# A tile of the token sums on the scan mask's place, priority for score copies, and a half-sum of the down weights moved to the branches

## The chip, the cores and the metric

The kernel runs on one core of a Trainium2 chip. TensorE (PE in the profile) multiplies matrices and writes to the PSUM banks; VectorE (DVE) and ScalarE (ACT) empty those banks and do the elementwise work; GpSimd (POOL) does elementwise work and issues part of the transfers; SyncE (SP) issues the rest. The engines run side by side and wait for each other through semaphores; each one works through its own queue strictly in order. The metric is the time of one execution on the device in microseconds; lower is better. A time "before" or "after" is a median over several runs.

## The reference

One decoder layer over 16 meta tokens and 1024 tokens of width 1024: a mixer with two branches (gated linear attention, GLA, and an mLSTM, 4 heads each) and a gated MLP with a width-3 causal convolution.

```python
def mixer_block(h, ...):
    proj = h @ w_in + b_in
    (g_q, g_k, g_v, g_r, g_lr, m_q, m_k, m_v, m_o, m_i, m_f, gate_a, gate_b) = split(proj)
    log_a = log_sigmoid(g_lr @ gla_w_gate + gla_b_gate) / GLA_TAU
    o_gla = head_rms(gla_chunked(g_q * dk**-0.5, g_k, g_v, log_a), gla_norm) * silu(g_r)
    mq, mk = split(silu(causal_dwconv(concat(m_q, m_k), ml_conv_w, ml_conv_b)))
    o_ml = head_rms(mlstm_chunked(mq * dk**-0.5, mk, m_v, m_i, log_sigmoid(m_f)), ml_norm) * sigmoid(m_o)
    y = sigmoid(gate_a) * (o_gla @ w_branch_gla) + sigmoid(gate_b) * (o_ml @ w_branch_ml)
    return y @ w_out
def conv_ffn(h, ...):
    gate, up = split(causal_dwconv(h @ w_up, conv_w, conv_b))
    return (silu(gate) * up) @ w_down
h = concat(meta, x)
h = h + mixer_block(rms_norm(h, norm_mix), ...)
h = h + conv_ffn(rms_norm(h, norm_ffn), ...)
return rms_norm(h, norm_final)[:, N_META:]
```

In the GLA scores, `scores[t, s] = sum_k q[t,k] k[s,k] exp(bc[t,k] - bc[s,k])` for `s <= t`, with `bc` the running sum of `log_a` within a chunk.

## The kernel before

**Stages.** Projections and heads first: head s = 0 to 3 is GLA, 4 to 7 mLSTM. While PE projects keys, queries and values of one head (matmuls `pj` and `pv`, lines 234, 263 and 276), the steps of the head before are mixed in as generators (`gla`, `mlstm`, then `post`). Then come the gates (`Vg`, `Xg`, `Yg`, `Zg`), the two branches (`bg`, `bm`), the output product (`po`), the second norm, the FFN's up products (`Vu` to `Zu`) and its down products (`pd`). Every matrix operand is split into a high and a low part (`wH`, `wL`; `xH`, `xL`), and three products are added.

**What sets the order.** A scheduler orders each engine's queue by priorities. `with hp(PRI_E)` raises the priority of what stands in it, mostly of the copies that empty a PSUM bank ("evictions"). `tc.issue_after(x)` puts a piece of work behind an instruction in the order. Tiles with the same tag share their buffers (`bufs` of them) in turn; a new tile waits until all users of the tile that held its buffer are done.

**Token sums.** The gates and the up product multiply block matrices with fewer products (sums of blocks are multiplied in place of single blocks). For the gates, sums of token blocks are made ahead on POOL: `token_sums(k)` writes four sums and differences into the halves of two tiles, `xa` and `xb`, and stores them to `tsc` in 8 transfers. It is called once early on (k = 0) and then in `post(4)`, `post(5)` and `post(6)`, that is while heads 5, 6 and 7 run. `xa` and `xb` have the tag `of` with two buffers, and so has `KT`, the transposed keys of a head: PE transposes keys into the banks `kt`, DVE scales them into `KT` (line 1101), and then PE's score products `msc` (line 1108) and the state updates `up` (line 1120) follow.

**The scan mask.** `rmask` (line 109) is ones with zeros at the starts of chunks. The scans that make running sums per chunk read it, last in `small_rows` (line 683), which runs beside the end of the GLA heads. After that it is not used.

**Half-sums.** `half_load` and `half_sums` (lines 644 to 658) load half a pair of rows of the down weights into a tile `ts`, make four differences on POOL and store them to `tdn`, for the down product much later. There are 22, taken in turn from the list `half`: three in `post(3)` to `post(5)`, five beside the last gates, seven in the `bg` steps, and the rest in the `bm` steps, one in each for as long as the list holds, on the place of the tiles `Y0` and `Y1` in turn. After the branches, the tokens' rows are loaded: `h1` onto `Y0` and `h2` onto `Y1` by POOL, the others by SP.

**GLA scores.** Within a chunk the score matrix is put together from halves of sizes 1, 2, 4 to 64 (`scores_small` for 1 to 16, `scores_large` for 32 and 64), and from the diagonal (`scores_diagonal`). `turn` flips the odd half by a product with `flip`. Each takes one of the three `s` banks of PSUM, whose next user waits for the copy out of it. In `small_rows`, lines 688, 692, 697 and 704 are DVE's sums on rows of 4 partitions (`sr` in the profile), and line 280 adds the bias to a projected value block (`v`), which frees a bank of `pj` and `pv`.

Of the kernel before, what the change touches and what calls it, by code (L numbers as in the profile page):

```python
# [9 lines left out]
F32 = mybir.dt.float32  # L10
F32R = mybir.dt.float32r
U8 = mybir.dt.uint8
AF = mybir.ActivationFunctionType
# [4 lines left out]
P = 128  # L18
# [3 lines left out]
T = NM + SEQ  # L22
# [23 lines left out]
def hybrid_kernel(ctx, tc, x, meta, norm_mix, w_in, b_in, gla_w_gate, gla_b_gate, gla_norm,  # L46
                  ml_conv_w, ml_conv_b, ml_norm, w_branch_gla, w_branch_ml, w_out, norm_ffn,
                  ffn_w_up, ffn_conv_w, ffn_conv_b, ffn_w_down, norm_final, out):
    nc = tc.nc
    x, out = x[0], out[0]  # L50
# [8 lines left out]
    def hp(n):  # L59

        return tc.high_priority(offset=max(1, min(n, tc.cur_priority - floor[0])))
# [9 lines left out]
    hd = heads_ctx.enter_context(tc.tile_pool(name="hd", bufs=1, side="right"))  # L71
# [32 lines left out]
    with tc.issue_after(loads[0]):  # L104
# [1 line left out]
    load_x(2)  # L106
    sent = nc.scalar.dma_start(m0[:, 1], bass.AP(tensor=norm_mix.tensor, offset=norm_mix.offset,
                                                 ap=[[P, NK], [0, NM], [1, P]]))
    rmask = hd.tile([P, T], F32, name="rmask")
    nc.vector.memset(rmask, 1.0)  # L110
    nc.vector.memset(rmask[:, 0:1], 0.0)
    nc.vector.memset(rmask[:, NM:].rearrange("p (n w) -> p n w", w=P)[:, :, 0:1], 0.0)
# [108 lines left out]
    PRI_W, PRI_E, PRI_Q, PRI_D, PRI_N = 2500, 2500, 600, 600, 400  # L221
# [92 lines left out]
    A = hd.tile([P, NC, P], F32, name="A", tag="A", bufs=1)  # L314
# [194 lines left out]
    with tc.issue_after(last.ins):  # L509

        lmask = {}
# [104 lines left out]
    def token_sums(k, queue):  # L616

        a, b = ([t[:, :514], t[:, 520:1034]] for t in (
            hd.tile([P, T], F32, name=f"x{i}{k}", tag="of", bufs=2) for i in "ab"))

        def whole(dst, i, c0):
            nc.gpsimd.tensor_tensor(dst, xH[:, i, c0:c0 + 514].bitcast(F32), xL[:, i, c0:c0 + 514].bitcast(F32), OP.add)

        def less(dst, x, y):
            nc.gpsimd.tensor_tensor(dst, x, y, OP.subtract)
        first, second = T0, T0 + 512
        whole(a[1], k, second)
        whole(a[0], k, first)
        less(b[0], a[1], a[0])
        whole(b[1], k + 4, second)  # L630
        less(a[1], b[1], a[1])
        less(b[1], b[1], b[0])
        whole(a[0], k + 4, first)
        less(a[0], a[0], b[1])
        for i, src in enumerate((b[0], b[1], a[1], a[0])):
            for p in range(2):
                stored = queue.dma_start(tsc[p][i, :, k], src[:, 258 * p:258 * p + 258 - 2 * p])
        return stored
# [15 lines left out]
    def half_sums(t, m, c):  # L654
        for o, a, b in ((0, 1, 0), (1, 3, 1), (3, 3, 0), (2, 2, 3)):
            nc.gpsimd.tensor_tensor(t[:, o], t[:, a], t[:, b], OP.subtract)  # L656
        for i in range(2):
            nc.gpsimd.dma_start(tdn[i][m][:, :, 256 * c:256 * c + 256], t[:, 2 * i:2 * i + 2])
# [71 lines left out]
    def post(s, oraw, om, sc):  # L730

        h = s % 4
        g = "g" if s < 4 else "m"
        after = rooted[0]
        if 4 <= s < 7:
            with tc.issue_after(after.ins):
                after = token_sums(s - 3, nc.gpsimd)
        for c in range(NC):
            o = oraw[c // 4][:, DV * (c % 4):DV * (c % 4 + 1)]
            nc.scalar.activation(o, o, AF.Copy, scale=sc[:, c + 1:c + 2])  # L740
        nc.scalar.activation(om, om, AF.Copy, scale=sc[:2, 0:1])
        nc.sync.dma_start(omd[g][h], om)
        for _ in range({3: 2, 6: 3}.get(s, 3)):
            yield
        dst = osc[g][2 * h:2 * h + 2].rearrange("t (q i) n -> i (t q) n", i=32)
        for j in range(2):
            t32 = hd.tile([P, T], F32, name=f"of{s}_{j}", tag="r", bufs=2)[:, :SEQ]
            with tc.issue_after(held[0]) if s > 2 else nullcontext():
                nc.vector.transpose(t32.rearrange("p (b c j) -> p c b j", b=8, c=4),
                                    oraw[j][:, :SEQ].rearrange("p (c b j) -> p c b j", c=4, b=8))  # L750
            yield
            if 3 <= s < 6:
                if j == 0:
                    with tc.issue_after(after.ins):
                        t = half_load(wp, "gst")
                else:
                    half_sums(*t)
            for a in range(4):
                nc.sync.dma_start(dst[:, :, 256 * a + P * j:256 * a + P * j + P],
                                  t32[32 * a:32 * a + 32].rearrange("p (b n) -> p b n", b=8))  # L760
            yield
# [54 lines left out]
    def gla(s):  # L816
# [7 lines left out]
        An = hd.tile([P, T], F32, name=f"An{s}", tag="of", bufs=2)  # L824
        raw = An[:, 512:SEQ]
        An = An[:, :512].rearrange("p (i t) -> p i t", t=P)
# [21 lines left out]
        def scores_diagonal(kq):  # L848

            for g in range(2):  # L850
                pt = ps.tile([P, 4, P], F32, name=f"sc{s}_0_{g}", tag="s", bufs=3)
                column_sums(pt, kq[g])
                nc.vector.copy_predicated(An if g else A.rearrange("p (i c) t -> p i c t", c=2)[:, :, 0, :],
                                          lmask[0][:, None, :].to_broadcast([P, 4, P]), pt)

        def turn():

            pt = ps.tile([P, 4, P], F32, name=f"sct{s}", tag="s", bufs=3)
            nc.tensor.matmul(pt, flip, A.rearrange("p (i c) t -> p i c t", c=2)[:, :, 1, :], start=True, stop=True)
            nc.scalar.activation(An, pt, AF.Copy)  # L860

        def products(pk, b):

# [8 lines left out]
        def scores_large(pk, b):  # L872
            m = 64 // b
            pt = products(pk, b)
            for c in range(2):
                A2 = An if c else A.rearrange("p (i c) t -> p i c t", c=2)[:, :, 0, :]
                for n in range(m):
                    p0 = b * (m * c + n)
                    nc.scalar.activation(A2[2 * b * n:2 * b * n + b, :, 2 * b * n + b:2 * b * (n + 1)],
                                         pt[p0:p0 + b, :, p0:p0 + b], AF.Copy)  # L880

        def scores_small(pk, b):
            pt = products(pk, b)
# [44 lines left out]
        for b in (1, 2, 4, 8, 16, 32, 64):  # L928
            made.append((b, level(b)))
            if len(made) > (3 if s == 0 else 2):  # L930
                c, pk = made.pop(0)
# [4 lines left out]
        if len(made) > 2:  # L936
            c, pk = made.pop(0)
# [4 lines left out]
        c, pk = made.pop(0)  # L942
# [35 lines left out]
        for g in range(2):  # L978
            tp = ps.tile([P, 4, P], F32, name=f"kt{s}_{g}", tag="s", bufs=3)
            for i in range(4):  # L980
                c = 4 * g + i
# [36 lines left out]
        for c2 in range(NC // 2):  # L1018
# [3 lines left out]
            for i in range(2):  # L1022
                c = 2 * c2 + i
# [8 lines left out]
            for i in range(2):  # L1032
                c = 2 * c2 + i
# [5 lines left out]
            for i in range(2):  # L1039
                c = 2 * c2 + i  # L1040
# [355 lines left out]
    for q in range(NG):  # L1396
        gu[q] = [row(f"gu0{q}", "u0", 2),
                 first_row if q == 1 else row(f"gu1{q}", "o1" if q % 2 else "u1")]
        for p in range(2):
            g = piece(psG, f"g{q}", p, gu[q], u2, WP[q], gate_block)  # L1400
# [85 lines left out]
    for j in END:  # L1486
        pt = prod3(ugb[j], [[t[:, k] for k in range(NK)] for t in (xH, xL)], False, f"pe{j}", 0, T0)
# [12 lines left out]
    for j in range(NK):  # L1500
# [4 lines left out]
        pt = prod3(ubg[j], og, j < 2, f"bg{j}")  # L1505
# [17 lines left out]
    for j in range(NK):  # L1523
# [7 lines left out]
        pt = prod3(ubm[j], om_, j < 1, f"bm{j}")  # L1531
# [24 lines left out]
    for t in range(NC + 1):  # L1556
        a = r2.tile([P, T], F32, name=f"h{t}", tag=f"Y{t - 1}") if t else rb.tile([P, T], F32, name="h0", tag="T12")
# [14 lines left out]
    for p in "HL":  # L1572
        t = rb.tile([P, 28, W0], F32R, name=f"B{p}0", tag=f"B{p}0")
# [213 lines left out]
    for i, tiles in enumerate(([1, 5, 2, 6, 0], [3, 7, 4, 8])):  # L1787
        for n in range(4):
# [13 lines left out]
            for it, t in enumerate(rest):  # L1802
                pt = po_bank(n, t, ("V1", "X1")[it % 2])
# [19 lines left out]
    for q in range(NJ):  # L1823
        for p in range(2):
            g = up_piece(q, p)
# [153 lines left out]
    t = r2.tile([P, 4, D], F32, name="accs", tag="OL1")  # L1979
# [121 lines left out]
    i = FIRST  # L2101
    while i < len(seq):
        r, ph, m = seq[i]
        k = i % NP2
# [3 lines left out]
        n = 4 if (r, ph, k) == (1, 1, NP2 - 4) else 2 if k in (0, NP2 - 2) else 1  # L2108
# [4 lines left out]
        if (r, ph) == (1, 0) and 2 <= k < 6:  # L2113
            scaled, x, rs = ready[k - 2]
# [46 lines left out]
```

## Time and profile before

| what | value |
|---|---|
| median of 3 runs | 1843.21 us (1843.0 to 1844.52) |
| the profiled execution | 1844.82 us |
| its span, first to last instruction | 1843.1 us |
| TensorE clock granted, mean | 0.999 |
| POOL busy in 0 to 600 us (heads) | 160.47 us |
| POOL busy in 870 to 1070 us (branches) | 100.59 us |
| PE idle in the first 40 us | 4.53 us |
| PE idle in the last 23 us | 8.2 us |

The page lists busy times per engine, the chain of work that ended last and the costliest groups of instructions. The chain goes through PE for 85% of the span, DVE for 6%, POOL, ACT and transfers for 2% each. A row of the timeline gives start, length, engine, line, operation, output and input, their shapes and how many instructions the row stands for; in brackets stands how long the engine was idle before it, and who ended that. "The old clock" is the time from the start of this profiled span.

### The profile page before, as it was taken

The numbers are of one execution on the slowest core, as the hardware profiler recorded it, in microseconds if no ns is written. First come the engines' busy times: TensorE is split into PE (matmuls) and PEld (weight loads), VectorE is DVE, ScalarE is ACT, GpSimd is POOL, SyncE is SP. The second block draws the span as 40 slices with busy tenths as digits, with TensorE's granted clock in tenths as the row PEclk, the third lists the DMA queues.
The fourth block names the chain that finished last, engine by engine and source line by source line (L and its number), as shares of the span: only waits on it lengthen the run. The fifth ranks groups of instructions, "written<-read, shape, count | busy, mean of one in ns | idle before, by whom it ended". The sixth has DMA issues, their size and how long they took to land.

```text
span 1843.1 us, 32483 instructions
## 1 busy us (share of the span) xinstructions
PE 1822.7 (99%) x13142; PEld 1756.9 (95%) x13142; DVE 1247.3 (68%) x1858; ACT 850.9 (46%) x1366; POOL 444.2 (24%) x511
## 2 busy tenths in 40 slices
PE   9999999999999999999999999999999999999998
PEld 8999999999999999999999999999999999988886
DVE  7966856656553566765613637798887887787876
ACT  6564564645434433332513235444434433465664
POOL 5400211205530011134462700013222222100100
PEclk9999999999999999999999999999999999999999
DMA  5212212224425354566963733333333334298894
GB/s 164 59 43 56 52 34 61 69 84 141 126 66 166 102 171 150 161 184 189 342 212 115 266 124 115 115 121 121 104 111 101 115 116 124 90 336 316 284 383 163
DMA packets 237469, 269.63 MB, mean 146 GB/s; under 512 B 15282, under 2 KB 194797, under 8 KB 237319
## 3 DMA queue, kind: packets, MB, share of 16 engines
q1 hardware_dynamic: 215583, 196.20, 34.4%
q0 software_dynamic: 19136, 62.62, 9.8%
q10 hardware_dynamic: 2600, 8.74, 1.3%
q8 instruction: 103, 1.69, 0.4%
q14 instruction: 47, 0.39, 0.1%
HBM read 197.91 MB, written 69.60 MB: 145 GB/s over the span
## 4 chain that ended last, share of the span: by engine, by line
PE 85%; DVE 6%; issue 3%; POOL 2%; ACT 2%; DMA 2%; SPq 0%; POOLq 0%; DVEq 0%; ACTq 0%
PE pj L234 8%; PE Yu L1218 7%; PE Zu L1218 7%; PE Xu L1218 7%; PE pv L276 5%; PE bg L1471 5%; PE bm L1471 5%; PE Zg L1218 4%; PE Yg L1218 4%; PE Xg L1218 4%; PE po L1765 4%; PE Vu L1218 3%; PE pdZ L1921 3%; PE pdX L1921 3%; PE pdY L1921 3%
## 5 line engine op out<-in xcount | busy, mean ns | idle before, releaser
L656 POOL TENSOR_TENSOR ts<-ts 128x256 f32<-128x256 f32 x88 | 81.9, 939 | 45.0 <-DMA ts<-in_ffn_w_down_dram 43.2
L1678 POOL TENSOR_TENSOR SB<-SA,rg 128x512 f32<-128x512 f32 x20 | 32.7, 1634 | 239.8 <-issue 101.4
L276 PE MATMUL pv<-wH_mv,xH 128*128 128x256 f32 x256 | 74.5, 291 | 0.1
L276 PE MATMUL pv<-wH_gv,xH 128*128 128x256 f32 x256 | 74.3, 290 | 0.0
L1765 PE MATMUL po<-wH_wo,yH 128*128 128x256 f32 x256 | 72.5, 283 | 0.1
L276 PE MATMUL pv<-wH_gv,xL 128*128 128x256 f32 x256 | 72.0, 281 | 0.0
L276 PE MATMUL pv<-wL_mv,xH 128*128 128x256 f32 x256 | 72.0, 281 | 0.0
L1765 PE MATMUL po<-wL_wo,yH 128*128 128x256 f32 x256 | 71.7, 281 | 0.3 <-DVE wL_wo L147 0.3
L276 PE MATMUL pv<-wL_gv,xH 128*128 128x256 f32 x256 | 71.9, 281 | 0.0
L276 PE MATMUL pv<-wH_mv,xL 128*128 128x256 f32 x256 | 71.9, 281 | 0.0
L1765 PE MATMUL po<-wH_wo,yL 128*128 128x256 f32 x256 | 71.8, 281 | 0.0
L1713 DVE SCALAR_TENSOR_TENSOR cv<-u,fc,cv 128x1024 f32<-128x1024 f32 x44 | 65.2, 1482 | 0.4
L920 POOL TENSOR_TENSOR pk<-pk,kT 128x256 f32<-128x256 f32 (+1 forms) x24 | 31.8, 1330 | 130.3 <-ACT pk L918 130.1
L1660 POOL TENSOR_TENSOR A<-u2raw,A 128x512 fp32r<-128x512 f32 x20 | 42.4, 2122 | 86.3 <-ACT A L1659 86.3
L1471 PE MATMUL bg<-ogL,wH_bg 128*128 128x342 f32 x192 | 61.5, 320 | 0.0
L1471 PE MATMUL bg<-ogH,wH_bg 128*128 128x342 f32 x192 | 61.5, 320 | 0.0
L1471 PE MATMUL bm<-omH,wH_bm 128*128 128x342 f32 x192 | 61.4, 320 | 0.0
L1471 PE MATMUL bm<-omH,wL_bm 128*128 128x342 f32 x192 | 61.3, 319 | 0.0
L1471 PE MATMUL bg<-ogH,wL_bg 128*128 128x342 f32 x192 | 61.3, 319 | 0.0
L1471 PE MATMUL bm<-omL,wH_bm 128*128 128x342 f32 x192 | 61.2, 319 | 0.0
L280 DVE TENSOR_TENSOR v<-pv,bB 128x256 f32<-128x256 f32 x64 | 26.6, 415 | 38.2 <-PE pv L276 38.0
L1659 ACT ACTIVATE HA<-rg 128x1024 fp32r<-128x1024 f32 x16 | 17.0, 1060 | 73.0 <-PE Yu L1218 72.6
(829 smaller groups left out, 7491.1 us busy)
## 6 DMA issues: line engine op xcount, KB each, us to landing
gw<-in_w_in_dram SPq DMA_DIRECT2D x26, 512.0 KB
ts<-in_ffn_w_down_dram POOLq DMA_DIRECT2D x44, 256.0 KB, 4.2
tdn<-ts POOLq DMA_DIRECT2D x44, 256.0 KB, 3.4
rg<-in_ffn_w_up_dram SPq DMA_DIRECT2D x22, 512.0 KB
ru<-in_ffn_w_up_dram SPq DMA_DIRECT2D x22, 512.0 KB
adr<-s SPq DMA_DIRECT2D x40, 256.0 KB
rd<-in_ffn_w_down_dram SPq DMA_DIRECT2D x20, 512.0 KB
do<-tdn SPq DMA_DIRECT2D x18, 512.0 KB
```

The source lines that it names most:

```text
L234: nc.tensor.matmul(pt[:, :n], a[:, k, :], b[:, k, base + t0:base + t0 + n], start=(i == 0), stop=(i == 3 * NK - 1))
L276: nc.tensor.matmul(pt[:, :DV], a[:, k, t0:t0 + P], b[:, k % 4, :], start=(i == 0), stop=(i == 3 * NK - 1))
L280: hold(nc.vector.tensor_tensor(vt[:n, c, :DV], pt[:n, :DV], bB[:n, :], OP.add).ins)
L656: nc.gpsimd.tensor_tensor(t[:, o], t[:, a], t[:, b], OP.subtract)
L920: eng.tensor_tensor(e, e, k, OP.mult)
L1218: nc.tensor.matmul(out[:, :n], x[:, k, :], y[:, k, :], start=start and k == 0 and j == 0, stop=stop and k == 3 and j == 2, skip_group_chec ...
L1471: nc.tensor.matmul(pt[:, i, :n], a[:, k, :], b[k][:, base + t0:base + t0 + n], start=(k == 0 and j == 0), stop=(k == NK - 1 and j == 2))
L1660: eng.tensor_tensor(l, src, h.bitcast(F32), OP.subtract)
L1678: late.tensor_tensor(sb[:, 0:4], sa[:, 0:4], rg[:, 0:4], OP.subtract)
L1713: nc.vector.scalar_tensor_tensor(y, u[:, j:SEQ + j], fc[:, j, jj:jj + 1], y, OP.mult, OP.add)
L1765: nc.tensor.matmul(pt[:, :DV], a, b[:, k % 4, :], start=(k == 0 and i == 0), stop=(k == NK - 1 and i == len(terms) - 1))
L1921: nc.tensor.matmul(banks[r, j, b][:, c], p, q[:, c], start=first and k == 0, stop=last and k == 2, skip_group_check=True)
```

## The change

Three edits; what is computed stays the same:

1. `rmask` gets a tag, `rm`, of its own with one buffer. In `token_sums(k)` with k > 0, `xb` takes that place in place of a buffer of the tag `of`; `xa` stays where it was. For k = 0 nothing changes.
2. The half-sum in `post(3)` is dropped (`3 <= s < 6` becomes `4 <= s < 6`). The list `half` keeps its 22 entries, so every later place takes the entry before, and the last step of the branches (`bm`, j = 7) now has one too, on the tile `Y1`.
3. The copies out of the banks in `turn`, `scores_diagonal` and `scores_large` get eviction priority, `hp(PRI_E)`.

```diff
-    rmask = hd.tile([P, T], F32, name="rmask")
+    rmask = hd.tile([P, T], F32, name="rmask", tag="rm", bufs=1)
...
         a, b = ([t[:, :514], t[:, 520:1034]] for t in (
-            hd.tile([P, T], F32, name=f"x{i}{k}", tag="of", bufs=2) for i in "ab"))
+            hd.tile([P, T], F32, name=f"x{i}{k}", tag=tag, bufs=2 if tag == "of" else 1)
+            for i, tag in (("a", "of"), ("b", "rm" if k else "of"))))
...
-            if 3 <= s < 6:
+            if 4 <= s < 6:
...
                 column_sums(pt, kq[g])
-                nc.vector.copy_predicated(An if g else A.rearrange("p (i c) t -> p i c t", c=2)[:, :, 0, :],
-                                          lmask[0][:, None, :].to_broadcast([P, 4, P]), pt)
+                with hp(PRI_E):
+                    nc.vector.copy_predicated(An if g else A.rearrange("p (i c) t -> p i c t", c=2)[:, :, 0, :],
+                                              lmask[0][:, None, :].to_broadcast([P, 4, P]), pt)
...
-            nc.scalar.activation(An, pt, AF.Copy)
+            with hp(PRI_E):
+                nc.scalar.activation(An, pt, AF.Copy)
...
-                    nc.scalar.activation(A2[2 * b * n:2 * b * n + b, :, 2 * b * n + b:2 * b * (n + 1)],
-                                         pt[p0:p0 + b, :, p0:p0 + b], AF.Copy)
+                    with hp(PRI_E):
+                        nc.scalar.activation(A2[2 * b * n:2 * b * n + b, :, 2 * b * n + b:2 * b * (n + 1)],
+                                             pt[p0:p0 + b, :, p0:p0 + b], AF.Copy)
```

On DVE, around the scaling of the keys of head 6 (`K0`, `A0` and `KT6` are written from the banks `k0t6` and `kt6`; in brackets stand the semaphores that a row waits for: DMASW are transfers that POOL issued), before:

```order
L749 STREAM_TRANSPOSE of5_1_5130<-or5_1_4736 128x4x8x32 [waits DMAHW6_49,DMAHW7_49,DMAHW5_49,DMAHW3_49]
L1093 TENSOR_SCALAR K0_436<-k0t6_5133,tcol_435 16x128 [waits PE_49]
L1094 TENSOR_SCALAR A0_437<-k0t6_5133,tcol_435 16x1
L1101 TENSOR_TENSOR KT6_5132<-kt6_0_5139,tcol_435 128x512 [waits DMASW1_49,DMASW6_49,DMASW0_49,DMASW7_49,PE_49,Pool_49]
L1101 TENSOR_TENSOR KT6_5132<-kt6_1_5145,tcol_435 128x512 [waits PE_49]
L147 TENSOR_TENSOR wL_mv3_1_5216<-wr_mv3_1_5213,wH_mv3_1_5215 128x1024 [waits DMAHW4_49,PE_49,Activation_49]
```

and with the change:

```order
L750 STREAM_TRANSPOSE of5_1_5121<-or5_1_4727 128x4x8x32 [waits DMAHW6_49,DMAHW7_49,DMAHW5_49,DMAHW3_49]
L1097 TENSOR_SCALAR K0_436<-k0t6_5124,tcol_435 16x128 [waits PE_49]
L1098 TENSOR_SCALAR A0_437<-k0t6_5124,tcol_435 16x1
L1105 TENSOR_TENSOR KT6_5123<-kt6_0_5130,tcol_435 128x512 [waits PE_49]
L1105 TENSOR_TENSOR KT6_5123<-kt6_1_5136,tcol_435 128x512 [waits PE_49]
L147 TENSOR_TENSOR wL_mv3_1_5207<-wr_mv3_1_5204,wH_mv3_1_5206 128x1024 [waits DMAHW4_49,PE_49,Activation_49]
```

The order of the rows stays; the first `KT6` no longer waits for transfers or for POOL. Heads 5 and 7 read the same way.

On POOL, at the end of GLA head 3 (`rs3r` is the root for its norm; `kT` and `qT` are the zeroed edges of later keys and queries), before:

```order
L700 MEMSET sr_3569 4x16
L124 TENSOR_TENSOR rs3r<-rs3v,mhalf 128x9
L650 DMA ts_3700<-in_ffn_w_down_dram 128x2x256 x2
L656 TENSOR_TENSOR ts_3700<-ts_3700 128x256 x3
L658 DMA tdn_432<-ts_3700 256x1x256
L656 TENSOR_TENSOR ts_3700<-ts_3700 128x256
L658 DMA tdn_433<-ts_3700 256x1x256
L592 MEMSET kT_4388 128x3
```

and with the change:

```order
L701 MEMSET sr_3569 4x16
L124 TENSOR_TENSOR rs3r<-rs3v,mhalf 128x9
L592 MEMSET kT_4379 128x3
L592 MEMSET kT_5047 128x3
L592 MEMSET qT_5048 128x3
```

The half-sum's two loads, four subtractions and two stores are gone from here.

On POOL, at the end of the branches (`h1` and `h2` are rows of tokens, `hr` roots of the second norm), before:

```order
L656 TENSOR_TENSOR ts100_10853<-ts100_10853 128x256
L658 DMA tdn1_433<-ts100_10853 256x1x256
L1561 DMA h1_11065<-in_x_dram 128x1024
L1561 DMA h2_11067<-in_x_dram 128x1024
L1596 TENSOR_TENSOR hr0_11574<-hv0_11572,mhalf_81 128x1
```

and with the change:

```order
L1565 DMA h1_11065<-in_x_dram 128x1024
L651 DMA ts101_11046<-in_ffn_w_down_dram 128x2x256 x2
L657 TENSOR_TENSOR ts101_11046<-ts101_11046 128x256 x3
L659 DMA tdn0_432<-ts101_11046 256x1x256
L657 TENSOR_TENSOR ts101_11046<-ts101_11046 128x256
L659 DMA tdn1_433<-ts101_11046 256x1x256
L1565 DMA h2_11067<-in_x_dram 128x1024
L1600 TENSOR_TENSOR hr0_11574<-hv0_11572,mhalf_81 128x1
```

A half-sum now stands between the two loads, and `h2` waits for its stores, since it takes the same place.

## The prediction

> **What bounds the kernel now.** I read the page first, for the engine that has no slack.
>
> ```profile
> span 1843.1 us, 32483 instructions
> PE 1822.7 (99%) x13142; PEld 1756.9 (95%) x13142; DVE 1247.3 (68%) x1858; ACT 850.9 (46%) x1366; POOL 444.2 (24%) x511
> ```
>
> PE works 1822.7 of 1843.1 us, and the change leaves every matmul in place. So only PE's idle 20.4 us can be won, and a loss can only be a new idle stretch of PE. The table of waits, for PE alone, says who makes it idle (us in total, times, longest):
>
> ```profile
> PE msc L1108 <- DVE KT L1101: 2.9, 2, 2.2
> PE pj L234 <- DVE v L280: 1.0, 1, 1.0
> PE sc L869 <- ACT An L860: 0.9, 1, 0.9
> ```
>
> The table of windows places the first two (after the window: its length, then busy time of PE, PEld, DVE, ACT, POOL, clock, DMA share, GB/s):
>
> ```profile
> 350.00:360.00 10.00, 9.03 (x67) 8.74 (x66) 9.81 (x10) 4.88 (x6) 5.83 (x6) 1.00 0.42 110
> 490.00:500.00 10.00, 9.36 (x61) 8.83 (x61) 6.04 (x8) 3.02 (x4) 4.41 (x5) 1.00 0.90 241
> 540.00:550.00 10.00, 7.79 (x62) 7.49 (x61) 4.33 (x8) 2.51 (x3) 2.42 (x5) 1.00 0.51 141
> ```
>
> The clock is granted in full, so a microsecond of idle is a microsecond, and the 2.21 missing in the last window are the longest wait of `msc` for `KT`.
>
> **Part 1, the token sums' second tile.** Why `KT` is late stands in DVE's timeline:
>
> ```profile
> 493.96 1.29 DVE L1101 TENSOR_TENSOR KT<-kt,tcol 128x512 f32<-128x512 f32 x2 [5.00 <-DMA tsc<-xb]
> 543.70 1.29 DVE L1101 TENSOR_TENSOR KT<-kt,tcol 128x512 f32<-128x512 f32 x2 [4.36 <-DMA tsc<-xb]
> ```
>
> DVE stands still for 5.00 and 4.36 us until the stores out of `xa` and `xb` have left, because `KT` takes a buffer of their pair. With `xb` on the mask's place, `KT` and `xa` each keep one of the two buffers, and the order of the changed program shows `KT` waiting for PE alone. What this costs PE is more than the wait itself, since the array drains and fills. I take it from start to start, against an undisturbed run of the same 16 matmuls in head 5:
>
> ```profile
> 442.33 1.95 PE L1108 MATMUL msc<-qc,kc 128*128 128x128 f32 x16
> 444.03 0.36 PE L263 MATMUL pv<-wH_mv,xM 128*128 128x256 f32 x1
> 493.01 1.05 PE L1108 MATMUL msc<-qc,kc 128*128 128x128 f32 x8
> 494.71 1.16 PE L1108 MATMUL msc<-qc,kc 128*128 128x128 f32 x8 [0.64 <-DVE KT L1101]
> 495.70 0.60 PE L1124 MATMUL u<-v,K 128*128 128x257 f32 x2
> 541.19 1.05 PE L1108 MATMUL msc<-qc,kc 128*128 128x128 f32 x8
> 544.45 1.16 PE L1108 MATMUL msc<-qc,kc 128*128 128x128 f32 x8 [2.21 <-DVE KT L1101]
> 545.36 0.36 PE L276 MATMUL pv<-wH_mv,xH 128*128 128x256 f32 x1
> ```
>
> Undisturbed: 444.03 - 442.33 = 1.70. Head 7: 545.36 - 541.19 = 4.17, so 2.47 lost. Head 6: 495.70 - 493.01 = 2.69, so 0.99 lost; another matmul follows there, so between the wait's 0.64 and 0.99, and I take 0.90. What is late next: without the wait `KT` of head 7 starts at 543.70 - 4.36 = 539.34 and ends 1.29 later at 540.6, before PE wants it (541.19 + 1.05 = 542.24); in head 6 at 488.96 to 490.25, against 494.06. Nothing takes the wait's place. The stores themselves stay on POOL where they are. **Term: -3.4 us, bounds -2.85 (the bare waits) and -3.5.**
>
> **Part 2, the half-sum that leaves the first mLSTM head.** Before it, around 355 us:
>
> ```profile
> 351.12 1.32 DVE L688 TENSOR_TENSOR sr<-raw_s,sr 4x1040 f32<-4x1040 f32 x1
> 354.06 2.33 DVE L692 TENSOR_TENSOR sr<-sr,sr 4x1040 f32<-4x1040 f32 x1
> 357.75 1.22 DVE L697 TENSOR_TENSOR sr<-sr,sr 4x1024 f32<-4x1024 f32 x1
> 359.00 0.42 DVE L280 TENSOR_TENSOR v<-pv,bB 128x256 f32<-128x256 f32 x1
> 349.90 3.97 POOL L656 TENSOR_TENSOR ts<-ts 128x256 f32<-128x256 f32 x3 [1.66 <-DMA ts<-in_ffn_w_down_dram]
> 354.46 0.82 POOL L656 TENSOR_TENSOR ts<-ts 128x256 f32<-128x256 f32 x1
> 358.19 0.32 PE L234 MATMUL pj<-xH,wL_mk 128*128 128x348 f32 x1
> 359.48 0.43 PE L234 MATMUL pj<-xH,wH_mk 128*128 128x346 f32 x1 [0.97 <-DVE v L280]
> 359.75 0.32 PE L234 MATMUL pj<-xL,wH_mk 128*128 128x346 f32 x1
> ```
>
> DVE has no gap there, and PE waits for `v`, the last row of that queue. L692 took 2.33 us while POOL's subtraction ran inside it; L697, of nearly the same size and free of POOL, took 1.22. Without the half-sum I expect L692 at about 1.22 (-1.11) and L688 at 1.22 (-0.10), so `v` ends at 359.42 - 1.21 = 358.21. PE's matmuls of this group follow each other every 0.16 us, so it would go on at 358.35: the wait just disappears. Its price, again start to start: 359.48 - 358.35 = 1.13 and a late second matmul (0.27 in place of 0.16), 1.24 in all. **Term: -1.1 us, bounds 0 (L692 is long for another reason) and -1.24.**
>
> The Trainium skill, VectorE: DVE Perf Modes, section Two Vector instructions with no wait between them, speaks against this term: an instruction whose operands start in another quarter of the partitions than those of the one before is held until that has finished. By this alone L692 stays long and the term is near 0, the whole sum -3.5. The trace speaks against it: L688 has operands that start in the same places as L692's and also stands behind a `v`, and took 1.32.
>
> **Part 3, where that half-sum goes.** It now stands on POOL between the loads of `h1` and `h2`, in the branches' last step.
>
> ```profile
> 1054.62 0.68 POOL L658 DMA_DIRECT2D tdn<-ts  x1 [0.30 <-POOL ts L656]
> 1057.72 0.54 POOL L1561 DMA_DIRECT2D h<-in_x_dram  x1 [0.69 <-DMA tdn<-ts]
> L656 POOL TENSOR_TENSOR ts<-ts 128x256 f32<-128x256 f32 x8 | 8.0, 1008 | 1.2 <-DMA ts<-in_ffn_w_down_dram 1.1
> ts<-in_ffn_w_down_dram POOLq DMA_DIRECT2D x5, 256.0 KB, 4.7
> tdn<-ts POOLq DMA_DIRECT2D x8, 256.0 KB, 4.0
> h<-in_x_dram POOLq DMA_DIRECT2D x2, 512.0 KB, 4.2
> 1076.65 1.13 DVE L1772 TENSOR_TENSOR h<-po,h 128x256 f32<-128x256 f32 x3 [1.99 <-PE po L1765]
> 1081.81 0.28 PE L1765 MATMUL po<-wH_wo,yH 128*128 128x256 f32 x1
> DMA to landing us min/median/max: 2.5/3.8/12.6
> ```
>
> On the old clock its loads start where `h2`'s did, at 1057.72: two issues of about 0.7, 4.7 to land, four subtractions of 1.0, two stores of 0.7, 4.0 to land, then `h2`: 0.54 and 4.2. That is 1057.72 + 1.4 + 4.7 + 4.0 + 1.4 + 4.0 + 4.7 = 1077.9, in place of 1062.5. Its reader is the third of the three sums that DVE does from 1076.65, at about 1077.4, so DVE may stand for half a microsecond. PE notices only when it needs the bank of a later sum behind that one, at 1081.81: some 3 us of cover. Two sums of about 0.4 lie between, so `h2` may land until about 1081.0. Behind it on POOL only the second norm's roots queue, which wait for all four column groups of the sums anyway. **Cost: 0; past 1081.0 each further microsecond of the landing is lost.**
>
> The Trainium skill, GPSIMD Engine Reference, section Specifications, says that POOL and VectorE share their SBUF interfaces and collide when VectorE reads two SBUF operands. It agrees with L692 above, and it warns here: if the subtractions slid 5 us later, they would meet the splits of the last branch tile; by my sum they are over at about 1068, before those splits begin, and the term stays 0.
>
> **Part 4, the copies with priority.** The order changes in head 0 alone: DVE takes the first diagonal copy ahead of `kq`'s split and the second behind the multiplication of `qh`; ACT takes `kh` between the copies, PE one column sum five matmuls later. For heads 1 to 3 all queues read as before, so the 0.94 us wait of `sc` for `An` in head 1 stays.
>
> ```profile
> 91.25 0.73 DVE L853 COPY_PREDICATED A<-mu,sc 128x512 f32<-128x512 uint8 x1
> 92.37 0.74 DVE L853 COPY_PREDICATED An<-mu,sc 128x512 f32<-128x512 uint8 x1 [0.38 <-PE sc L840]
> 91.87 0.39 PE L840 MATMUL sc<-kq,ones 128*128 128x512 f32 x1
> ```
>
> The split is one copy (about 0.65 us) later and so is its matmul; the second copy ends some 0.7 us later, and the readers of both are covered by PE's projection of `v`. **Cost 0, bounds ±0.2.**
>
> **Sum.** -3.4 - 1.1 + 0 + 0 = -4.5 us of the profiled execution's 1844.82, which gives 1840.3. The median of the runs shown is 1843.21, 1.6 below that execution, so the median after should be **1838.7**. 0.2% (3.7 us), about what a measurement of this kernel can tell from no change, is only just behind the forecast.
>
> **Rivals.**
> - *The wait for `v` stays* (L692 was not POOL's doing, or the 0.14 us of slack is missed): only part 1 works, 1843.2 - 3.4 = 1839.8, inside 0.2%. For it: the slack is thin. Against it: 2.33 beside 1.32 and 1.22. Chance 0.22.
> - *The gain is partly given back*: after 360 us POOL's and DVE's work meet at other moments; one more collision like L692's costs about 1.1, two 2.2. With all terms this gives 1839.8 to 1841. Also here: `KT` freed from the stores and caught by something else (only part 2 left, 1842.1), against which its list of waits speaks. Chance 0.12.
> - *Slower: `h2` is late.* One landing in this stage took 12.6 us, where the median is 3.8. The loads and the stores of the new half-sum are two landings in a row. From a landing of `h2` at 1081.0 + 4.5 = 1085.5 on the old clock all gains are gone, from 1089.2 the kernel is slower by over 0.2%; both landings at 12.6 would put it at 1077.9 + 7.9 + 8.6 = 1094.4, PE idle for 13.4, and the time at 1852. Against it: the medians of this window, 4.7 and 4.0, leave it at 1077.9. Chance 0.05.
> - *More*: the wait in head 1 goes too (-0.94), 1837.7. Chance 0.03.
>
> **How the numbers follow.** The forecast has 0.58. Faster by over 0.2%: 0.58 + 0.03 and a part of those given back little, 0.62. Within 0.2%: 0.33. Slower: 0.05. The range runs from the bounds of all terms with the extra wait (1837.0) to two collisions on top of the bare part 1 (1841.5).
>
> **What would show it.** Right: DVE's idle time before `KT` names no DMA, PE's windows 490:500 and 540:550 are full, L692 is at about 1.2 us and the row of `pj` waiting for `v` is gone; DVE's third sum in the `po` stage waits for `h` for less than a microsecond. Wrong: a new row in PE's table of waits, most likely `po` behind `h`, or L692 at 2.3 without POOL beside it.

## The result and the profile after

| | before | after |
|---|---|---|
| median, us | 1843.39 (8 runs, 1842.88 to 1845.13) | 1838.91 (8 runs, 1837.17 to 1842.1) |
| profiled execution: time, span | 1844.82, 1843.1 | 1838.80, 1837.1 |
| PE idle in the span | 20.4 | 16.7 |

The ratio is 0.9975 with a 95% interval of 0.9964 to 0.9985: the changed kernel is 4.5 us faster by the medians, within 2.8 and 6.6. A second group of runs gave 1838.61 beside 1843.46 (0.9974, 0.9964 to 0.9985). The forecast was 1838.7.

The head of the page after, and the two longest rows of PE's table of waits that are not of the start-up (after each pair: us in total, times, longest):

```profile
span 1837.1 us, 32479 instructions
PE 1820.4 (99%) x13142; PEld 1754.7 (96%) x13142; DVE 1243.0 (68%) x1858; ACT 850.6 (46%) x1366; POOL 442.7 (24%) x511
```
```profile
PE sc L872 <- ACT An L863: 1.0, 1, 1.0
PE htp L1617 <- DVE hs L1596: 0.6, 1, 0.6
```

Of the 6.0 us between the two spans, 3.7 are idle time of PE and 2.3 are time in which it counts as busy. The rows of `msc` waiting for `KT` and of `pj` waiting for `v` are gone; that of `sc` for `An`, which the prediction left standing, stands. The windows at the three places (after the window: its length, then busy time of PE, PEld, DVE, ACT, POOL, clock, DMA share, GB/s):

```profile
350.00:360.00 10.00, 10.00 (x72) 9.92 (x72) 9.78 (x11) 5.80 (x6) 0.00 (x0) 1.00 0.26 58
490.00:500.00 10.00, 10.00 (x62) 9.26 (x62) 8.31 (x11) 6.10 (x8) 5.79 (x7) 1.00 0.87 256
540.00:550.00 10.00, 10.00 (x62) 9.47 (x62) 4.60 (x10) 4.53 (x10) 0.00 (x0) 1.00 0.56 151
```

All three are full. DVE's timeline at the first place and at the two `KT` shows what made them so (start, duration, operation, and in brackets the idle time ahead and who ended it):

```profile
349.96 1.23 DVE L689 TENSOR_TENSOR sr<-raw_s,sr 4x1040 f32<-4x1040 f32 x1
352.81 1.23 DVE L693 TENSOR_TENSOR sr<-sr,sr 4x1040 f32<-4x1040 f32 x1
356.66 0.42 DVE L280 TENSOR_TENSOR v<-pv,bB 128x256 f32<-128x256 f32 x1
486.08 1.29 DVE L1105 TENSOR_TENSOR KT<-kt,tcol 128x512 f32<-128x512 f32 x2
535.40 1.27 DVE L1105 TENSOR_TENSOR KT<-kt,tcol 128x512 f32<-128x512 f32 x2
```

L693, L692 of before, takes 1.23 us in place of 2.33, and `KT` has no idle time ahead of it in place of 5.00 and 4.36 us behind the stores.

**Where the time went, place by place.** If the start of each PE matmul after is taken from the start of the same matmul before, the lead of the changed kernel grows in steps and is flat between them: 1.15 at 30 us (before any edited instruction has run), 2.35 behind head 4's `v`, 2.88 behind 453 us in head 5, 3.9 in head 6, 6.34 behind head 7's `KT`, and 6.34 still at 1050. So the steps are 1.2 (forecast 1.1), 0.5 (not forecast), 1.0 (forecast 0.9) and 2.47 (forecast 2.47). The lead at the end is 1.5 more than the medians differ: one pair of executions holds chance as well, and which steps belong to the change is what the experiments had to say.

### The profile page after: what moved, and what is told of

Same layout as the page of the kernel before. It is cut to its first block, busy times and chain, and to the rows that moved or that the text cites. A ratio compares the mean times of both kernels' runs of the same rounds, so it can differ in the third digit from the quotient of the medians.

```text
span 1837.1 us, 32479 instructions
## 1 busy us (share of the span) xinstructions
PE 1820.4 (99%) x13142; PEld 1754.7 (96%) x13142; DVE 1243.0 (68%) x1858; ACT 850.6 (46%) x1366; POOL 442.7 (24%) x511
## 4 chain that ended last, share of the span: by engine, by line
PE 87%; DVE 6%; DMA 3%; ACT 2%; issue 2%; POOL 1%; SPq 0%; POOLq 0%; DVEq 0%; ACTq 0%
PE pj L234 10%; PE pv L276 8%; PE Yu L1222 7%; PE Zu L1222 7%; PE Xu L1222 7%; PE bg L1475 5%; PE bm L1475 5%; PE Zg L1222 4%; PE Yg L1222 4%; PE Xg L1222 4%; PE po L1769 4%; PE Vu L1222 3%; PE pdZ L1925 2%; PE pdX L1925 2%; PE pdY L1925 2%; PE Vg L1222 2%
```

## The experiments

The leads of every profiled kernel against the first profile of before, read in the same way, are collected here; the runs are told below. "Old" and "new" say where the token sums' second tile is, "half-sum" whether it is still in the first mLSTM head. Each column is what that execution gained at the place (negative: lost).

| kernel profiled | start, 30 us | head 4, `v` | head 5, 453 us | head 6, `KT` | head 7, `KT` |
|---|---|---|---|---|---|
| before, again (old, half-sum) | 0.3 | 0 | 0.5 | 0.7 | -1.8 |
| before, third (old, half-sum) | 1.0 | 0 | 0.2 | 0.2 | -0.1 |
| priority only (old, half-sum) | 2.2 | 0 | 0.4 | 0.65 | 0 |
| half-sum only (old, moved) | 2.7 | 1.2 | 0.5 | 1.0 | -1.6 |
| token sums only (new, half-sum) | 1.9 | 0 | 0.3 | 1.0 | 2.47 |
| after (new, moved) | 1.15 | 1.2 | 0.5 | 1.0 | 2.47 |
| after, again (new, moved) | 0.6 | 1.2 | 0.4 | 1.0, then -0.8 | 2.47 |

**Each part alone.** Part 1, made in the kernel before:

```diff
-    rmask = hd.tile([P, T], F32, name="rmask")
+    rmask = hd.tile([P, T], F32, name="rmask", tag="rm", bufs=1)
...
-            hd.tile([P, T], F32, name=f"x{i}{k}", tag="of", bufs=2) for i in "ab"))
+            hd.tile([P, T], F32, name=f"x{i}{k}", tag=tag, bufs=2 if tag == "of" else 1)
+            for i, tag in (("a", "of"), ("b", "rm" if k else "of"))))
```

> The kernel before with part 1 alone (the token sums' second tile on the mask's place). My theory: of the four steps by which the changed kernel's trace pulls ahead of the one before (1.20 us at head 4's wait for v, 0.54 in head 5, 1.02 in head 6, 2.43 in head 7) this one has the last two, because KT no longer stands behind the stores out of xb, and, if the half-sum of head 5 starts sooner for the same reason, the 0.54 too: 3.5 to 4.0 us in all, 1839.4 to 1839.9 beside 1843.4. L692 stays at 2.3 us and PE keeps its wait of 1.0 for v. Rival (the stores were not what KT waited for, or something else catches KT): DVE still stands 2 us or more ahead of KT in heads 6 and 7, and the time stays within 1 us of the kernel before. Rival for head 5 (its 0.54 comes from the half-sum that left head 4): the wait of op for om, 0.49, is still there.

Measured: 1839.27 beside 1843.38 (ratio 0.9976, 0.9967 to 0.9985), 4.1 us faster. DVE's rows and PE's remaining wait:

```profile
352.14 2.32 DVE L693 TENSOR_TENSOR sr<-sr,sr 4x1040 f32<-4x1040 f32 x1
486.73 1.29 DVE L1102 TENSOR_TENSOR KT<-kt,tcol 128x512 f32<-128x512 f32 x2
536.01 1.27 DVE L1102 TENSOR_TENSOR KT<-kt,tcol 128x512 f32<-128x512 f32 x2
```
```profile
PE pj L234 <- DVE v L280: 0.9, 1, 0.9
```

`KT` is free and the wait for `v` is not: the 2.47 of head 7 are part 1's, the 1.2 of head 4 are not. Head 5's wait shrank from 0.49 to 0.18 us.

Parts 2 and 3 alone:

```diff
-            if 3 <= s < 6:
+            if 4 <= s < 6:
```

> The kernel before with parts 2 and 3 alone (one half-sum from the first mLSTM head's surroundings to the branches). My theory: L692 falls from 2.33 to about 1.23 us, the wait of pj for v goes, one step of 1.2 us at 356; the waits of msc for KT (0.64 and 2.21) stay; in the sum with h2 DVE waits 0.5 to 0.9 us for the load and PE for nothing: 1842.2 beside 1843.4. Rival (L692 was long for another reason and part 1 gave the 1.2): L692 stays at 2.3, the time as before. Rival (h2 late costs PE): a wait of po in PE's table and a time at or above that of before.

Measured: 1842.43 beside 1843.38 (0.9994, 0.9985 to 1.0004), which the rounds can't tell from nothing; the trace can. Its row of L692 and its wait for `KT`:

```profile
351.26 1.23 DVE L692 TENSOR_TENSOR sr<-sr,sr 4x1040 f32<-4x1040 f32 x1
```
```profile
PE msc L1108 <- DVE KT L1101: 2.3, 1, 2.3
```

The step of 1.2 is there and the wait for `v` gone, as expected. Two things are not as expected. DVE does not wait for `h2` at all. And the table has one wait for `KT`, not two: head 6's is gone, though the tile is in its old place.

Part 4 alone, the priority on the copies:

```diff
-            nc.scalar.activation(An, pt, AF.Copy)
+            with hp(PRI_E):
+                nc.scalar.activation(An, pt, AF.Copy)
...
```

> The kernel before with part 4 alone (the three copies with eviction priority; the order of the program differs in head 0 only). My theory: nothing, 1843.4 within 0.2 us of the shift between its trace and that of before from 85 us to the end of the heads; the wait of sc for An in head 1, 0.94, stays. Rival (the start-up shift of 1.15 us that the changed kernel shows at 25 us, or part of the later steps, comes from the copies): 1 us or more faster.

Measured: 1844.59 beside 1843.38 (1.0005, 0.9996 to 1.0014). In the trace the lead over before is 2.2 at 45 us and 2.2 at 440: no step at the copies, so part 4 is worth nothing here. Its median leans to the slow side by 1.2 us, which the interval does not tell from zero. Again one wait for `KT` only, 2.2 us in head 7.

**The kernel before, twice more.** Was head 6's wait a property of the kernel?

> The kernel before, profiled once more. In the profiles of the two kernels that kept the old tile (the half-sum alone, the priority alone) the wait of msc for KT in head 6 did not come, and that of op for om in head 5 neither; only that in head 7 did. My theory: these two depend on when the stores land and are not in every execution of the kernel before; head 7's wait (2.2) and the wait for v (1.0) are in every one. The start up to 25 us is also not the same in each: I expect this execution 1 to 2.7 us ahead of the first one at 25 us. Rival: the order that the other kernels changed removed the waits, and all four waits are here again.

Measured: 1844.44 us. The waits of 1.0 for `v` and for `An` are here again, those in heads 5 and 6 are not, so the theory holds on these. The start was expected 1 to 2.7 us ahead of the first profile and was 0.3 ahead: a miss. And head 7 cost more than in the first profile, 1.8 us more in the lead, of which only 0.4 is a longer wait. The rest shows in windows of 1 us there; the seventh number behind the window, next to the last two, is the granted clock:

```profile
542.00:543.00 1.00, 0.00 (x0) 0.00 (x0) 0.38 (x1) 0.00 (x0) 0.00 (x0) 1.00 0.95 255
543.00:544.00 1.00, 0.64 (x3) 0.64 (x4) 1.00 (x3) 0.00 (x0) 0.00 (x0) 0.56 0.77 276
544.00:545.00 1.00, 1.00 (x6) 1.00 (x6) 0.83 (x2) 0.00 (x0) 0.00 (x0) 0.50 0.12 37
545.00:546.00 1.00, 1.00 (x7) 1.00 (x6) 0.52 (x1) 0.00 (x0) 0.00 (x0) 0.50 0.00 0
546.00:547.00 1.00, 1.00 (x8) 1.00 (x7) 0.17 (x1) 0.00 (x0) 0.00 (x0) 0.73 0.00 0
547.00:548.00 1.00, 1.00 (x11) 1.00 (x10) 0.00 (x0) 0.55 (x1) 0.00 (x0) 1.00 0.00 0
```

PE is busy all the time from 544 on, but issues 6 to 8 matmuls a microsecond where 11 are usual: after the wait the clock is at half speed. What is missing to 1.00 adds up to 0.44 + 0.50 + 0.50 + 0.27 = 1.71 us, 3.4 us at half; a part of it falls into the wait itself, and 1.5 (1.84 less 0.37) is what PE lost by it. The kernel with the half-sum alone had the same behind its wait (0.33 + 0.50 + 0.50 + 0.38 = 1.71 in its windows from 540 to 544, and 1.6 in the lead, 0.1 of it a longer wait); the priority kernel and the first profile of before did not. So another execution was taken to see whether the length of the wait decides:

> The kernel before, profiled a third time. Four profiles of kernels with the old tile place show a wait of msc for KT in head 7 of 2.21, 2.23, 2.29 and 2.58 us; after the two longer ones the granted clock is 0.50 for some 3.4 us and 1.7 us more are lost, after the two shorter ones it stays at 1.00. My theory (the length of the idle time decides, with an edge near 2.25): if this run's wait is 2.25 or less, no row of windows below 1.00 from 535 to 555; if longer, 0.50 for 3.4 us behind it. Rival (chance of the moment, not the length): a wait above 2.3 without a drop, or one below 2.2 with it. Head 6's wait: there in one of four so far, expected absent.

Measured: 1843.22 us, a wait of 2.28 us in head 7 and a clock of 1.00 throughout. So an edge at 2.25 falls. The five waits were 2.21, 2.23 and 2.28 (no drop), 2.29 and 2.58 (drop). Head 6's wait was there though it was expected absent, 0.4 us with 0.8 lost against the kernels that have none: it comes in some executions, 0 to 1.0 us lost, by when the stores land.

The traces themselves say what decides. In each profile all changes of the clock lie whole multiples of 3.413 us apart: in before, again at 543.12, at 546.54 (one step later) and, behind the last matmul, at 1836.78 (378 more). The place of these steps differs from execution to execution; the change behind the last matmul fixes it where the clock did not drop earlier (1837.64 in the first profile of before). Here is the step that holds the largest part of head 7's wait, in order for before, before third, priority only, half-sum only and before again:

```profile
540.58:543.99 3.41, 1.66 (x15) 1.47 (x13) 0.29 (x1) 0.00 (x0) 1.84 (x4) 1.00 0.96 271
538.73:542.14 3.41, 2.08 (x19) 1.89 (x17) 0.00 (x0) 0.00 (x0) 2.30 (x5) 1.00 0.93 248
539.70:543.11 3.41, 1.88 (x16) 1.88 (x17) 2.62 (x5) 0.00 (x0) 0.00 (x0) 1.00 0.70 199
536.93:540.35 3.42, 1.22 (x10) 1.22 (x11) 1.97 (x4) 0.00 (x0) 0.11 (x1) 1.00 0.83 242
539.71:543.12 3.41, 1.07 (x10) 0.88 (x8) 0.50 (x1) 0.00 (x0) 1.31 (x3) 1.00 0.97 257
```

PE is idle there for 1.75, 1.33, 1.53, 2.20 and 2.34 us, and only behind the last two is the clock at 0.50 for the next step. The same holds in all 14 profiles, from where the record of the clock begins (6 to 19 us) to the end: the clock halved behind each of the 22 full-speed steps in which PE was idle for 1.85 us or more, and behind none in which it was idle for 1.82 or less. So it is the length and the moment together: how much of the wait falls into one step.

**What lengthens L692.** Three dummies at the half-sum's old place in the changed kernel. First, loads and subtractions, no stores:

```diff
+            if s == 3 and j == 0:
+                with tc.issue_after(after.ins):
+                    ...
+                    for k in range(2):
+                        nc.gpsimd.dma_start(dt[:, 2 * k:2 * k + 2], ...)
+            if s == 3 and j == 1:
+                for d, x, y in ((0, 1, 0), (1, 3, 1), (3, 3, 0), (2, 2, 3)):
+                    nc.gpsimd.tensor_tensor(dt[:, d], dt[:, x], dt[:, y], OP.subtract)
```

> The changed kernel with a dummy half-sum at the old place in the first mLSTM head: its two loads and four subtractions on POOL, without the two stores; its result is not used and the eight real half-sums stay where the change put them. My theory (POOL's subtractions lengthen DVE's): L693, now 1.23 us, is 2.3 again, L689 1.32, and PE waits for v by 0.9 to 1.0 again; 1.2 us slower than the changed kernel in the trace's shift at 356. Rival (the stores, or the queue's transfers, were what lengthened it): 1.23 and no wait.

Measured: 1838.57 us in its one run. DVE's and POOL's rows:

```profile
349.55 1.32 DVE L689 TENSOR_TENSOR sr<-raw_s,sr 4x1040 f32<-4x1040 f32 x1
352.49 1.71 DVE L693 TENSOR_TENSOR sr<-sr,sr 4x1040 f32<-4x1040 f32 x1
348.30 4.82 POOL L762 TENSOR_TENSOR tsd<-tsd 128x256 f32<-128x256 f32 x4 [1.63 <-DMA tsd<-in_ffn_w_down_dram]
```

Half a hit: longer, but by 0.48 and not by 1.1. The four subtractions end at 348.30 + 4.82 = 353.12, 0.63 us into L693. PE lost 0.58 against the changed kernel, just the 0.48 and the 0.09 of L689. Second, the transfers alone:

```diff
+            if s == 3 and j == 1:
+                for i in range(2):
+                    nc.gpsimd.dma_start(scr[:, 2 * i:2 * i + 2], dt[:, 2 * i:2 * i + 2])
```

> The changed kernel with the transfers of a dummy half-sum at the old place, two loads and two stores of the loaded data to a scratch tensor, without the subtractions. My theory (the subtractions, not the transfers): L693 stays at 1.23 us, no wait of PE for v, shift against the changed kernel 0 across 356. Rival (transfers): 2.3 and the wait.

```profile
354.53 1.23 DVE L694 TENSOR_TENSOR sr<-sr,sr 4x1040 f32<-4x1040 f32 x1
```

1841.22 us in its one run, most of the difference from a start-up that is 1.7 us behind the changed kernel's at 24 us; no step at 356. The transfers alone cost nothing (their issues on POOL were over by 352.27; one that lies in L694 itself was not tried alone). Third, all of it, with the first store between the third and the fourth subtraction as in the kernel before:

> The changed kernel with a whole dummy half-sum at the old place: two loads, four subtractions, two stores to a scratch tensor, in the order that the kernel before has them. With the subtractions alone L693 took 1.71 us, since without the first store ahead of it the fourth subtraction was over at 353.12, 0.63 us into L693. My theory: what counts is how long a subtraction of POOL lies in L693; with the store between the third and the fourth, the fourth moves into L693 whole, L693 takes 2.3, L689 1.3, PE waits for v by about 1.0 and 1.1 to 1.2 us are lost at 356. Rival (in the kernel before something other than this half-sum added the rest): 1.7 and 0.6 us lost.

```profile
348.56 1.32 DVE L690 TENSOR_TENSOR sr<-raw_s,sr 4x1040 f32<-4x1040 f32 x1
351.50 2.20 DVE L694 TENSOR_TENSOR sr<-sr,sr 4x1040 f32<-4x1040 f32 x1
351.85 0.75 POOL L763 TENSOR_TENSOR tsd<-tsd 128x256 f32<-128x256 f32 x1
```
```profile
PE pj L234 <- DVE v L280: 0.8, 1, 0.8
```

1837.96 us in its one run; the subtraction now lies whole in L694, which takes 2.20, and PE lost 1.06 at 357: 0.97 of L694 and 0.09 of L690. That is the wait for `v` of the kernel before, put back. The three lengths follow one rule: the row ends 1.08 to 1.11 us after the end of the subtraction that lies in it. That is 354.46 + 0.82 = 355.28 and 354.06 + 2.33 = 356.39 in the kernel before, 353.12 and 354.20 with the subtractions alone, 352.60 and 353.70 here.

**How late `h2` may be.** The last two half-sums of the branches both in the last step, on one tile and so one behind the other:

```diff
-        if half:
-            half_sums(*half_load(r2, f"Y{j % 2}"))
+        for _ in range(0 if j == NK - 2 else 2 if j == NK - 1 else 1):
+            if half:
+                half_sums(*half_load(r2, f"Y{j % 2}"))
```

> The changed kernel with the last two half-sums of the branches both in the last step, one behind the other on one tile, so that the load of h2 stands behind two round trips in place of one. By the changed kernel's rows (first loads issued at 1053.12, h2's load at 1066.28, its reader at 1071.80) the second round trip takes another 13.2 us, h2 is there at about 1085. My theory, by the limit that the prediction gave (landing at 1081.0 on the old clock, 1074.7 on this one, costs PE nothing, and each microsecond past it one): PE idle for about 10 us in the output projection, a new row of po waiting for DVE's h, 1849 us. Rival (PE has other work to do there, or the sums are not what frees its banks): less than 3 us lost, below 1842. Rival (the stage holds less cover than I gave it): 12 us or more, above 1851.

Measured: 1846.66 beside 1842.95 (1.002, 1.0011 to 1.003), some 7.9 us above the changed kernel. PE's wait, the sums on DVE, and windows around them:

```profile
PE po L1770 <- DVE h L1777: 5.5, 1, 5.5
```
```profile
1076.28 0.56 POOL L1566 DMA_DIRECT2D h<-in_x_dram  x1 [3.90 <-DMA tdn<-ts]
1080.05 1.08 DVE L1777 TENSOR_TENSOR h<-po,h 128x256 f32<-128x256 f32 x3 [9.27 <-DMA h<-in_x_dram]
1080.86 0.58 PE L1770 MATMUL po<-wH_wo,yH 128*128 128x256 f32 x1 [5.51 <-DVE h L1777]
```
```profile
1084.00:1085.00 1.00, 1.00 (x5) 1.00 (x6) 1.00 (x2) 0.00 (x0) 0.00 (x0) 0.50 0.04 11
1085.00:1086.00 1.00, 1.00 (x7) 1.00 (x7) 0.26 (x1) 0.51 (x2) 0.00 (x0) 0.56 0.90 291
1086.00:1087.00 1.00, 1.00 (x11) 1.00 (x10) 0.35 (x1) 0.00 (x0) 0.00 (x0) 1.00 0.72 254
```

None of the three theories had all of it. The place and the limit are right: PE stopped at 1080.86 - 5.51 = 1075.35 and went on 0.81 us after DVE's sums began, so `h2` landing by 1075.35 - 0.81 = 1074.5 would have cost nothing; by the leads (0.29 and 6.34) that is 1081.2 on the clock of before, where the prediction said 1081.0. The landing came at 1080.05 and not at 1085, since the first round trip started 2.7 us sooner and `h2` took 3.8 and not 5.5 us from its issue. But the price is wrong: 5.5 us of idle time cost 7.9 in the lead, since the clock is at 0.50 until about 1085.9 behind it.

**A version without the wait in head 1.** Why does the wait for `An` in head 1 stand in spite of the priority? PE's matmul that makes the turned scores was over by 153.6, and `An`'s copy came at 158.55, behind four other instructions on ScalarE. The likely reason, which no run tests by itself, is that the scheduler goes by its own model of the times and ranks by priority only what it takes for ready. So the order was set by hand in the changed kernel, with `turn()` handing back its copy:

```diff
-        turn()
+        turned = turn()
...
-        nc.scalar.activation(kh, kh, AF.Exp, scale=1.0 / 16)
+        with tc.issue_after(turned.ins) if s == 1 else nullcontext():
+            nc.scalar.activation(kh, kh, AF.Exp, scale=1.0 / 16)
```

> The changed kernel with the exponential of kh in head 1 made to wait for the copy of the turned scores, which puts the splitting of gv's weights and that copy ahead of it on ScalarE. My theory of why the priority did nothing in head 1: the scheduler ranks what it takes for ready, and it takes the turned scores for late, so a priority can't lift their copy; an order by hand can. Then the copy starts at about 157.0 in place of 158.55, PE wants it at 158.34, and the wait of 0.95 goes: a step of 0.9 us at 160 and 1838.0 beside 1838.9. Rival: something else holds that matmul (kh's product on DVE, 0.9 us later, delays the predicated copies), and less than 0.3 us is left of it.

ScalarE's rows in the changed kernel, then in this one, and the window 150 to 170 of both:

```profile
156.50 1.07 ACT L960 ACTIVATE kh<-kh 128x1040 f32<-128x1040 f32 x1 [0.55 <-DVE kh L959]
157.48 1.05 ACT L146 ACTIVATE wH_gv<-wr_gv 128x1024 fp32r<-128x1024 f32 x1
158.55 0.60 ACT L863 ACTIVATE An<-sct 128x512 f32<-128x512 f32 x1
150.00:170.00 20.00, 19.05 (x132) 17.84 (x130) 11.81 (x19) 9.79 (x17) 0.00 (x0) 1.00 0.21 60
```
```profile
156.30 1.04 ACT L146 ACTIVATE wH_gv<-wr_gv 128x1024 fp32r<-128x1024 f32 x1
157.37 0.60 ACT L863 ACTIVATE An<-sct 128x512 f32<-128x512 f32 x1
157.86 1.06 ACT L961 ACTIVATE kh<-kh 128x1040 f32<-128x1040 f32 x1
150.00:170.00 20.00, 20.00 (x139) 19.11 (x139) 12.99 (x20) 10.42 (x20) 0.00 (x0) 1.00 0.21 60
```

PE is full there, the row of `sc` for `An` is gone, and the lead over the changed kernel grows by 1.2 at 159, where 0.9 was expected. Time: 1837.11 beside 1843.38 (0.9969, 0.9958 to 0.9981). Then both once more on one chip:

> The changed kernel once more, beside the next one on the same chip. 1838.9 within 0.7; no wait of msc for KT, of pj for v or of op for om in its table; the wait of sc for An, 0.9 to 1.0, is there. Start-up up to 25 us within 2 us of the first execution.

> The changed kernel with the copy of the turned scores put ahead of the exponential of kh by hand, timed on the same chip as the changed kernel. By its first profile the wait of sc for An is gone and the step is 1.2 us: 1.2 us below the changed kernel, ratio to it 0.9993, which rounds like these can see only as a tendency. Rival: chance of the first call; the same median within 0.3 us.

Measured: the changed kernel 1838.61 (0.9974), this one 1837.12 (0.9966, 0.9954 to 0.9978), and the step of 1.2 at 159 again. It beats the kernel before clearly. Against the changed kernel the 1.5 us between the medians are less than the intervals can tell, but the step is in both traces. The changed kernel's second profile also had what its expectation ruled out: `op` waited 0.6 us for `om`, now in head 6.

## Why the prediction was right, and what in it was not

The forecast of 1838.7 and its range held, and the steps of the two main terms were right in mechanism and place. Point by point:

- **Part 1, head 7: right.** 2.47 were forecast and 2.47 are the step in all three profiles with the new place.
- **Part 1, head 6: right in the pair, wrong as a term.** The prediction priced a single execution's wait at 0.90, as a property of the kernel. In that execution it was 1.0; the five profiles of kernels with the old place lost 1.0, 0.3, 0.8, 0.4 and 0 us there (before, again, third, priority only, half-sum only), 0.5 in the mean.
- **"The clock is granted in full, so a microsecond of idle is a microsecond": this step failed.** It held for the execution on which the prediction was made. In two of five with the old place, head 7's wait was followed by 3.4 us at half clock, and 1.8 and 1.6 us more were lost, 0.7 in the mean of the five. The change removes these with the wait: from 30 to 1830 us the clock is at 1.00 throughout in both profiles of the changed kernel. By these five profiles the waits that part 1 removes cost 2.47 + 0.5 + 0.7 = 3.7 us, beside a term of 3.4: head 6 was priced 0.4 too high, and the clock, at nothing, 0.7 too low. That the sum still fits so well is in part luck.
- **Part 2: right.** 1.1 was forecast, 1.2 measured; POOL's subtractions and not its transfers make L692 long: it ends about 1.1 us after the subtraction that lies in it. The Trainium skill, VectorE: DVE Perf Modes, section Two Vector instructions with no wait between them, by whose rule L692 would have stayed long, does not bear on it: with the same operands and the same `v` ahead, L693 takes 1.23 us.
- **Part 3: right, with some luck in the landing.** DVE waited 0.73 us for `h2` in the first profile after, until 1071.80, which is 1078.1 on the old clock where 1077.9 was forecast; the load was issued 0.6 us sooner than in the sum and landed 0.8 us later behind its issue. In the second profile DVE did not wait at all; PE never did. Past the limit a microsecond is dearer than the prediction had it: 7.9 us for 5.5.
- **Part 4: right.** No step where the copies are.
- **The range: its ends don't follow from the sums named for them.** All bounds with the extra wait give 1843.2 - 5.9 = 1837.3 and not 1837.0; the bare 2.85 of part 1 with two collisions gives 1843.2 - 2.85 + 2.2 = 1842.6 and not 1841.5, which is the sum with one. The measured median lies inside either way.
- **Not forecast: head 5.** `op` waited for `om` there before (0.49) and not after. DVE's split ahead of `om` took 1.78 us before and 1.23 to 1.67 in the others, by how POOL's half-sum falls on it: 0.2 to 0.5 us were gained there in every profile of the table, those of the kernel before included. It is chance of the first profile, not the change.

Summed from the places that the runs attribute: 1.2 for `v`, 2.47, 0.5 and 0.7 for `KT`, together 4.9 us, beside 4.5 and 4.9 by the medians of the two groups. Not settled is how much of the 0.7 another group of runs would show. An estimate: if the place of the clock's steps is chance, a wait of 2.2 to 2.6 us has 1.85 of it in one step in (3.41 + wait - 2 x 1.85) / 3.41, that is 0.56 to 0.68, of the executions, and at 1.5 us each that is 0.8 to 1.0 us in the mean.

## What to carry to other kernels

A wait in one profile is one draw: before a term is priced from it, see by which event it ended, and profile the kernel before once more. Here head 6's wait for the stores took 0 to 0.64 us in the five profiles with the old tile place, while the wait for `v`, behind DVE's queue, took 0.94 to 0.98 in all five with the half-sum at its old place. An idle stretch of PE can cost more than its length, by how much of it falls into one step of the clock. Tile places that two users share turn one user's slow stores into the other's wait, and giving one of them a place that was out of use by then cost nothing here. Where a priority doesn't move an instruction, an explicit "issue after" can, as it did in head 1.

## What was not expected of the hardware

- The clock is set in steps of 3.413 us whose place differs from execution to execution. In the 14 profiles a step with 1.85 us or more of PE idle time was followed by half clock (0.50), one with 1.82 or less was not (PE's times are modelled, so the edge is good to a few hundredths at best). A wait of 2.29 us was followed by it and one of 2.28 us was not, by where they fell; after 5.5 us it lasted until about 5 us after PE's restart, over the rest of the step of the restart and one full step. The Trainium skill, TensorE: Matmul & The Clock Gate, section Part 1: The HAM clock gate (the "warmup" mystery), has the half clock come after an idle window of about 3.4 us and last until about as long a busy one is over. The length of the window and the second half agree with the 3.413 us measured; that the whole window is idle does not, since 1.85 us in one step were enough here, and the measurement decides.
- A POOL subtraction and a DVE subtraction with two inputs take turns; they do not share. The DVE rows at L692 take 1.23 us alone and otherwise end 1.08 to 1.11 us after the POOL subtraction in them, so 1.71, 2.20 and 2.33 us. L688's 1.32 is the same: the first of the row of three ended at 351.34, 1.10 us before L688's end. POOL is held likewise: one of its subtractions took 0.73 us alone (at 1057.67 in the profile after), but the first two of the row of three, beside `kc` and L688, 1.45 and 1.63. Which of the two goes first is not shown: L692 began 0.40 us ahead of the subtraction and was held all the same.
- Up to 30 us, before any edit acts, executions of nearly the same program differ by up to 3.3 us (0.6 behind the first profile of before, with the transfers alone, to 2.7 ahead of it, with parts 2 and 3 alone). In one pair of profiles that is more than most of the terms here.
